# Sums of the down weight's quarters: from SBUF accumulation between products to DRAM copies and accumulating transfers during gate and up

## The chip, the cores and the metric

The program runs on one NeuronCore of one Trainium2 chip. The metric is device time in microseconds (us); less is better. The engines are named as in the profile: PE multiplies matrices (PEld is its weight load), DVE is VectorE, ACT is ScalarE, POOL is GpSimd, and SP issues most DMA transfers (SPq is its DMA queue, POOLq is POOL's).

## The reference, cut to what matters

Two decoder layers work on 512 tokens of width 1024 in float32. Each is a mixer, a layer norm, a dense SwiGLU feed-forward network (FFN) and a second layer norm. Only the FFN is touched:

```python
def swiglu(x, w_gate, w_up, w_down):
    return (jax.nn.silu(x @ w_gate) * (x @ w_up)) @ w_down
...
    for layer in range(DEPTH):
        ...
        x = layer_norm(ALPHA * x + y, ln_mix_g[layer], ln_mix_b[layer])
        x = layer_norm(ALPHA * x + swiglu(x, w_gate[layer], w_up[layer], w_down[layer]), ...)
```

The hidden width is 2816, in 22 tiles of 128 features. All weights are read from DRAM once per layer.

## The kernel before

**Products in three matmuls.** Each float32 operand is split into a rounded part `hi`, copied by ACT, and a remainder `lo`, which DVE makes as source minus `hi` (`split`, L98). A product is then three matmuls: hi by hi, hi by lo, lo by hi.

**Gate and up.** The first two hidden tiles are plain. The other twenty go in ten pairs of tiles, each by a scheme of seven block products in place of eight (`sevens`, L649). `make(i)` readies the weight operand of product i, and `take(i)` issues its 24 matmuls of 256 columns (L712). A pair of tiles needs four quarters of weight, fetched by SP into the pool `rawp`, which has `RAW` = 5 buffers of 512 KB; DVE forms the sums of quarters that the scheme needs (L684, L690).

**Down.** Sixteen of the 22 hidden tiles go through a second scheme of seven (`seven_down`, L524). There are four groups of tiles (q = 0 to 3), and for each a 2 by 2 block of weight quarters "11", "12", "21" and "22" of 512 KB each. The seven positions (`pos`) need these weights: 1 takes 11; 2 takes 21; 3 takes 22; 5 takes 11+12; 6 takes 11+12+22; 4 takes 11+12+22+21; 7 takes 22+12. That is 28 products, in the order of `seq` (L542). `make(i)` splits the weight (ACT then DVE), forms the activation combination on DVE where the position asks for one (positions 5, 6, 3 and 7, L580 to L588) and splits that too. `take(i)` issues 12 matmuls of 512 columns (L609); after the last group of a position it also copies the PSUM result away (L615, L619, L624) or combines it (L628, L631).

**Where the sums of weight quarters came from.** A buffer `tsum` in SBUF first holds quarter 11. Once `make` of position 1 has split it, POOL issues a DMA that adds quarter 12 into that same buffer (L559); once position 5 has split it, 22 is added; once position 6 has, 21. In the same way 12 is added into the buffer of 22 between positions 3 and 7. These buffers take the SBUF room of `xh` and `xl`, the split FFN input, which gate and up read to their end. The first two loads for down (quarter 21 of q = 0 and 1, at -3 and -2 in `loads`, L562) are issued inside the call of `seven_down`, before the gate and up loop goes past its seventh product.

**Order.** In the FFN the order on every engine is that of the program (`tc.manual_schedule`, L465): `make(i)`, then `take(i - AHEAD)` with `AHEAD` = 4 (L509 to L520). So what `take(i - 4)` puts on ACT and DVE stands behind what `make(i)` puts there. A split weight occupies one of `WP` = 5 pairs of buffers until its product has been taken. After the 28 products, `down` (L332) multiplies the remaining six hidden tiles plainly (L345) and runs the layer norm.

Of the kernel before, what the change touches and what calls it, by code (L numbers as in the profile page):

```python
# [10 lines left out]
F32 = mybir.dt.float32  # L11
F32R = mybir.dt.float32r
U8 = mybir.dt.uint8
AF = mybir.ActivationFunctionType
ALU = mybir.AluOpType
AX = mybir.AxisListType

P = 128
S = 512
NB = S // P  # L20
D = 1024
# [15 lines left out]
QUADS = 4  # L37
# [9 lines left out]
def trunk(ctx, tc, a, out):  # L47
    nc = tc.nc
# [7 lines left out]
    big = ctx.enter_context(tc.tile_pool(name="big", bufs=1))  # L56
    rawp = ctx.enter_context(tc.tile_pool(name="rawp", bufs=RAW))
# [4 lines left out]
    sm = ctx.enter_context(tc.tile_pool(name="sm", bufs=4))  # L62
    sm2 = ctx.enter_context(tc.tile_pool(name="sm2", bufs=2))
    sm1 = ctx.enter_context(tc.tile_pool(name="sm1", bufs=1))
    psp = ctx.enter_context(tc.tile_pool(name="psp", bufs=8, space=bass.MemoryType.PSUM))

    cnt = [0]

    def nm(s):
        cnt[0] += 1  # L70
        return f"{s}{cnt[0]}"

    def slot(dt=F32):
        return wk.tile([P, 512], dt, tag="wk", name=nm("wk"))

    def slot2(dt=F32):
        return hx.tile([P, 512], dt, tag="hx", name=nm("hx"))

    def temp(tag="tmp", dt=F32):
        return tmp.tile([P, 512], dt, tag=tag, name=nm(tag))  # L80
# [4 lines left out]
    def ps():  # L85
        return psp.tile([P, 512], F32, tag="ps", name=nm("ps"))
# [11 lines left out]
    def split(src, hi, lo, pool=False):  # L98
        nc.scalar.copy(out=hi, in_=src)  # L99
        if pool:  # L100
            n = src.shape[1] // 2
            for c in (slice(0, n), slice(n, 2 * n)):
                nc.gpsimd.tensor_tensor(out=lo[:, c], in0=src[:, c], in1=hi[:, c].bitcast(F32), op=ALU.subtract)
            return
        tt(out=lo, in0=src, in1=hi.bitcast(F32), op=ALU.subtract)  # L105
# [19 lines left out]
    xh, xl = [], []  # L125

    def renew():
        for t, n in ((xh, "xh"), (xl, "xl")):
            t[:] = [big.tile([P, 4, S], F32R, tag=f"{n}{j}", name=nm(n)) for j in range(2)]

    def xk(t, k, cols=slice(0, S)):
        return t[k // 4][:, k % 4, cols]
# [313 lines left out]
    def ffn(layer, last, flips):  # L446
        hs = []
        m8 = {}

        def hidden_tile(f):  # L450
            if f < WK:
                return slot()
            if not m8:
                m8["t"] = big.tile([P, 8, S], F32, tag="m8", name=nm("m8"))
            return m8["t"][:, f - WK, :]

        def finish(f, pg, pu):
            h = hidden_tile(f)
            t = temp()
            act(out=t, in_=pg, func=AF.Silu)  # L460
            tt(out=h, in0=t, in1=pu, op=ALU.mult)
            hs.append(h)

        E = mybir.EngineType
        with tc.manual_schedule(engines={E.PE, E.Activation, E.DVE, E.Pool, E.SP}):  # L465
            first, sx = [], {}

            def lower(flip):
                w, bank = first[-1]
                gemm_a(bank, w, cols=slice(0, 256), ks=range(4))  # L470
                if flip:
                    flips.pop(0)()
                gemm_a(bank, w, cols=slice(0, 256), ks=range(4, KD))

            def upper(f):
                for w, bank in first[2 * f:2 * f + 2]:
                    gemm_a(bank, w, cols=slice(256, 512))

            ready = state["ready"]
            for i in range(4):  # L480
                first.append((ready.pop(0), ps()))
                if i < 2:
                    ready.append(weight())
                if i == 3:
                    total, make, take, n = sevens(sx, hs, hidden_tile)
                    total(1)
                lower(i % 2)
            s1, s2_sum, s2, s3, s4 = sums(sx)
            s1()
            make(0)  # L490
            upper(0)
            finish(0, first[0][1], first[1][1])
            s2_sum()
            upper(1)
            make(1)
            make(2)
            finish(1, first[2][1], first[3][1])
            s2()
            make(3)
            take(0)  # L500
            s3()
            make(4)
            s4()
            make(5)
            take(1)
            take(2)
            make(6)
            acc, more, takes = seven_down(hs)
            for i in range(AHEAD + 3, n + len(more) + AHEAD):  # L509
                if i < n:  # L510
                    make(i)
                elif i < n + len(more):
                    more[i - n]()
                    if i == n + 3:
                        gb = load_ln("ffn", layer)
                i -= AHEAD
                if i < n:
                    take(i)
                else:
                    takes[i - n]()  # L520
        rest = [h for h in hs[:DIRECT]] + [h for h in hs[DIRECT + 2 * QUADS:]]
        return down(rest, [1, 5], gb, last, acc=acc)

    def seven_down(hs):  # L524
# [3 lines left out]
        base = state["i"]  # L528
        state["i"] += 4 * QUADS
        raw, ops = {}, {}  # L530
        t_, s_ = {}, {}

        def room(q):

            if q % 2 == 0:
                t = big.tile([P, 2, D], F32, tag=f"xh{q // 2}", name=nm("tsum"))
                s = big.tile([P, 4, 512], F32, tag=f"xl{q // 2}", name=nm("ssum"))
                for j in range(2):
                    t_[q + j], s_[q + j] = t[:, j, :], s[:, j, :]

        g = {}
        seq = [(2, 0), (2, 1), (1, 0), (1, 1), (2, 2), (5, 0), (1, 2), (5, 1), (1, 3), (2, 3), (5, 2), (6, 0),  # L542
               (5, 3), (6, 1), (6, 2), (6, 3), (3, 0), (3, 1), (3, 2), (3, 3), (7, 0), (7, 1), (7, 2), (7, 3),
               (4, 0), (4, 1), (4, 2), (4, 3)]

        def piece(which, q):
            i = base + 4 * q + ("11", "12", "21", "22").index(which)
            return a["w"][i // 2, :, (i % 2) * D:(i % 2) * D + D]

        def load(which, q):  # L550
            if which == "11":
                room(q)
                nc.sync.dma_start(out=t_[q], in_=piece(which, q))
                return
            raw[which, q] = rawp.tile([P, D], F32, tag="raw", name=nm("raw"))
            nc.sync.dma_start(out=raw[which, q], in_=piece(which, q))

        def add(t, which, q):
            nc.gpsimd.dma_start(out=t, in_=piece(which, q), accum_op=ALU.add)  # L559

        loads = {}
        for at, args in ((-3, ("21", 0)), (-2, ("21", 1)), (0, ("11", 0)), (1, ("11", 1)), (2, ("21", 2)),  # L562
                         (4, ("11", 2)), (5, ("11", 3)), (6, ("21", 3)), (12, ("22", 0)), (13, ("22", 1)),
                         (14, ("22", 2)), (15, ("22", 3))):
            loads.setdefault(at, []).append(args)

        def make(i):

            for args in loads.get(i, ()):
                load(*args)  # L570
            pos, q = seq[i]
            (a11, a21), (a12, a22) = hs[DIRECT + q], hs[DIRECT + QUADS + q]
            w = raw["21", q] if pos == 2 else raw["22", q] if pos in (3, 7) else t_[q]
            hi, lo = pair()
            split(w, hi, lo)
            if pos in (1, 5, 6, 3):
                add(w, {1: "12", 5: "22", 6: "21", 3: "12"}[pos], q)
            hh, hl = slot2(F32R), slot2(F32R)
            x = {1: a11, 2: a12, 4: a22, 7: None}.get(pos, s_.get(q))
            if pos == 5:  # L580
                tt(out=x, in0=a22, in1=a21, op=ALU.subtract)
            elif pos == 6:
                tt(out=x, in0=x, in1=a11, op=ALU.add)
            elif pos == 3:
                tt(out=x, in0=x, in1=a12, op=ALU.subtract)
            elif pos == 7:
                x = temp()
                tt(out=x, in0=a11, in1=a21, op=ALU.subtract)  # L588
            if pos == 6:
                act(out=hh, in_=x, func=AF.Copy, scale=-1.0)  # L590
                stt(out=hl, in0=x, scalar=-1.0, in1=hh.bitcast(F32), op0=ALU.mult, op1=ALU.subtract)
            else:
                split(x, hh, hl)
            ops[i] = hi, lo, hh, hl
# [38 lines left out]
        acc = {}  # L633
# [4 lines left out]
            acc.update({b: [g["a"][b], g["d"][b]] for b in range(2)})  # L638
            acc.update({b + 2: [g["f"][b], g["e"][b]] for b in range(2)})

        for at in range(-3, 0):
            for args in loads.get(at, ()):
                load(*args)
        n = len(seq)
        takes = [lambda i=i: take(i) for i in range(n)]
        takes[-1] = lambda: last(lambda: take(n - 1))
        return acc, [lambda i=i: make(i) for i in range(n)], takes

    def sevens(sx, hs, hidden_tile):  # L649

# [786 lines left out]
```

## Time and profile before

| | |
|---|---|
| three runs | 1088.09, 1090.30, 1090.39 us; median 1090.3 us |
| the profiled execution | 1089.05 us, span 1087.2 us from first to last instruction |
| PE busy (matmul) | 1049.5 us, 97% of the span |
| DVE busy | 791.2 us, 73% |
| ACT busy | 544.1 us, 50% |
| POOL busy | 89.2 us, 8% |
| mean granted PE clock | 0.986 of full speed |
| HBM read and written | 119.83 MB and 2.10 MB |

PE is busy nearly all the time, so only the places where it isn't, or where its clock is lower, can give time. Times in the rows are counted from the span's start. The down products of layer 0 run from 400 to 494 us, those of layer 1 from 953 to 1047 us.

### The profile page before, as it was taken

Reading aid. Unit: us, or ns where it says so; the run is one execution under the profiler, and the core shown is the slowest. Engines: PE = TensorE matmul, PEld = TensorE weight load, DVE = VectorE, ACT = ScalarE, POOL = GpSimd, SP = SyncE. Lnnn points to the kernel's source line nnn. Section 1 sums busy time; section 2 is a strip of 40 time slices with the busy share of each in tenths; the row PEclk is TensorE's granted clock in tenths of the full one; section 3 lists DMA queues with packets and bytes.
Section 4 is the critical chain, followed back from the end, with each engine's and each line's share of the span. In section 5 each row is a group of like instructions: output and inputs, shape, how many; then the busy total and the mean of one; then the engine's idle time right before and its main releaser. Section 6 shows DMA issues by size and latency. Waiting matters only on the chain.

```text
span 1087.2 us, 17047 instructions
## 1 busy us (share of the span) xinstructions
PE 1049.5 (97%) x6861; PEld 947.1 (87%) x6861; DVE 791.2 (73%) x1180; ACT 544.1 (50%) x896; POOL 89.2 (8%) x130
## 2 busy tenths in 40 slices
PE   9999999999999999599999999999999999997797
PEld 7888889999999997488988888889999999985686
DVE  5666549887877876685857886488887887776767
ACT  5544335655555454464467554356555554544541
POOL 0000000000000001200513411000000000022001
PEclk9999999999999999899999999999999999998899
DMA  9522222324333359833242031223424324398502
GB/s 335 201 75 79 78 78 72 97 93 129 97 102 114 98 161 256 138 101 99 97 137 77 2 117 43 78 73 79 124 90 137 97 85 130 117 255 154 133 20 78
DMA packets 35536, 123.04 MB, mean 113 GB/s; under 512 B 3952, under 2 KB 4608, under 8 KB 35456
## 3 DMA queue, kind: packets, MB, share of 16 engines
q1 hardware_dynamic: 30560, 104.12, 29.3%
q0 software_dynamic: 4896, 17.83, 9.3%
q8 instruction: 54, 0.88, 0.3%
q14 instruction: 26, 0.21, 0.1%
HBM read 119.83 MB, written 2.10 MB: 112 GB/s over the span
## 4 chain that ended last, share of the span: by engine, by line
PE 86%; DVE 5%; DMA 5%; ACT 3%; issue 1%; SPq 0%; POOL 0%; DVEq 0%; ACTq 0%; POOLq 0%
PE ps L712 35%; PE ps L189 15%; PE ps L345 13%; PE ps L609 7%; PE ps L223 6%; DMA tsum<-in_w_dram 4%; DVE w L105 2%; ACT w L99 2%; PE ps L1161 1%; PE ps L285 1%; PE ps L1086 1%; PE ps L1009 1%; PE ps L858 1%; PE ps L805 1%; PE ps L845 1%
## 5 line engine op out<-in xcount | busy, mean ns | idle before, releaser
L105 DVE TENSOR_TENSOR w<-raw,w 128x1024 fp32r<-128x1024 f32 (+2 forms) x174 | 210.0, 1211 | 60.3 <-ACT w L99 55.7
L712 PE MATMUL ps<-xh,w 128*128 128x256 f32 x1280 | 237.5, 283 | 0.0
L99 ACT CAST w<-raw 128x1024 fp32r<-128x1024 f32 (+3 forms) x177 | 181.4, 1032 | 65.7 <-PE ps L712 18.1
L712 PEld LDWEIGHTS ps<-xh,w 128*128 128x128 f32 x1280 | 202.7, 192 | 0.0
L609 PE MATMUL ps<-w,hx 128*128 128x512 f32 x672 | 159.9, 400 | 27.9 <-ACT ps L619 23.5
L712 PE MATMUL ps<-xl,w 128*128 128x256 f32 x640 | 181.1, 283 | 0.0
L609 PEld LDWEIGHTS ps<-w,hx 128*128 128x128 f32 x672 | 129.1, 193 | 58.1 <-ACT ps L619 24.4
L712 PE MATMUL ps<-hx,w 128*128 128x256 f32 x1440 | 179.6, 283 | 0.0
L712 PEld LDWEIGHTS ps<-hx,w 128*128 128x128 f32 x1440 | 176.0, 192 | 0.1
L189 PE MATMUL ps<-xh,w 128*128 128x512 f32 (+1 forms) x608 | 161.2, 348 | 0.4 <-ACT w L99 0.4
L345 PE MATMUL ps<-w,hx 128*128 128x512 f32 x657 | 151.9, 391 | 0.0
L345 PEld LDWEIGHTS ps<-w,hx 128*128 128x128 f32 x657 | 122.7, 188 | 25.1
L712 PEld LDWEIGHTS ps<-xl,w 128*128 128x128 f32 x640 | 122.8, 192 | 0.3
L189 PEld LDWEIGHTS ps<-xh,w 128*128 128x128 f32 x608 | 106.3, 189 | 15.9 <-ACT w L99 0.8
L189 PE MATMUL ps<-xl,w 128*128 128x512 f32 (+1 forms) x304 | 104.9, 345 | 0.0
L189 PEld LDWEIGHTS ps<-xl,w 128*128 128x128 f32 x304 | 57.6, 190 | 6.7 <-DVE xl L105 0.3
L559 POOL DMA_DIRECT2D tsum<-in_w_dram x24 | 20.9, 871 | 493.4 <-DVE w L105 282.1
L223 PE MATMUL ps<-w,xh 128*128 128x512 f32 (+1 forms) x192 | 58.6, 386 | 0.3 <-ACT lng L1065 0.3
L105 DVE TENSOR_TENSOR w<-tsum,w 128x1024 fp32r<-128x1024 f32 x32 | 39.2, 1224 | 18.1 <-ACT w L99 18.1
L105 DVE TENSOR_TENSOR w<-lng,w 128x1024 fp32r<-128x1024 f32 x30 | 36.7, 1223 | 17.1 <-ACT w L99 16.9
L105 DVE TENSOR_TENSOR w<-lnb,w 128x1024 fp32r<-128x1024 f32 x30 | 36.7, 1223 | 15.0 <-ACT w L99 14.9
L105 DVE TENSOR_TENSOR hx<-m,hx 128x512 fp32r<-128x512 f32 x32 | 21.4, 689 | 31.8 <-ACT hx L99 31.8
(250 smaller groups left out, 1285.4 us busy)
## 6 DMA issues: line engine op xcount, KB each, us to landing
raw<-in_w_dram SPq DMA_DIRECT2D x166, 512.0 KB, 4.3
tsum<-in_w_dram POOLq DMA_DIRECT2D x24, 512.0 KB, 8.4
raw<-in_w_dram POOLq DMA_DIRECT2D x10, 512.0 KB, 5.7
tsum<-in_w_dram SPq DMA_DIRECT2D x8, 512.0 KB, 6.3
hx<-in_xT_dram SPq DMA_DIRECT2D x8, 256.0 KB, 6.2
xn<-in_xn_dram SPq DMA_DIRECT2D x4, 512.0 KB, 9.4
out_dram<-xn SPq DMA_DIRECT2D x7, 256.0 KB, 2.0
lng<-in_ln_mix_g_dram SPq DMA_DIRECT2D x2, 512.0 KB, 7.7
```

The costliest lines, as they stand in the source:

```text
L99: nc.scalar.copy(out=hi, in_=src)
L105: tt(out=lo, in0=src, in1=hi.bitcast(F32), op=ALU.subtract)
L189: mm(dst[:, cols], lhsT=l[:, k, :], rhs=xk(r, k, cols), start=(k == 0 and n == 0), stop=(k == KD - 1 and n == 2))
L223: mm(banks[b][:, :n], lhsT=xk(l, k, t), rhs=r[:, c], start=(k == 0 and m == 0), stop=(k == KD - 1 and m == 2))
L285: nc.tensor.transpose(tp[:, k * P:(k + 1) * P], xn[:, b, h * 512 + k * P:h * 512 + (k + 1) * P], ident)
L345: mm(acc[b][h], lhsT=l(b), rhs=r[:, h * 512:h * 512 + 512], start=(not begun and k == 0 and n == 0), stop=(k == ends[b, h] and n == 2), sk ...
L559: nc.gpsimd.dma_start(out=t, in_=piece(which, q), accum_op=ALU.add)
L609: mm(bank, lhsT=l[:, t], rhs=r[:, c], start=(fresh and k == 0 and m == 0), stop=(k == 1 and m == 2), skip_group_check=True)
L712: mm(bank[:, f * 256:f * 256 + 256], lhsT=l[:, f, k, :], rhs=r[k // 2][:, k % 2, :], start=(start and f == 0 and k == 0 and m == 0), stop= ...
L805: mm(banks[s][bank][:, o:o + n], lhsT=l[rows[s], b * P:(b + 1) * P], rhs=r[rows[s], (b + 1) * P - n:(b + 1) * P], start=(i == 0), stop=(i ...
L845: nc.tensor.transpose(bank[:, o:o + P], src, ident)
L858: mm(po[rows[s], b * P:(b + 1) * P], lhsT=vn[:, j * P + 64 * s:j * P + 64 * s + 64], rhs=loc[s][(b, half)], start=(half == 0 or b == 0), s ...
```

## The change

The sums are no longer built in SBUF between products. For each q, four DRAM tiles `t` are made: t1 = 11+12, t2 = t1+22, t4 = t2+21, t3 = 22+12. Each comes from a DRAM to DRAM copy and one accumulating DMA into DRAM, both issued by POOL: 32 transfers of 512 KB per layer, kept in the list `steps`, of which one is put into the program after the `make` of gate and up product i where i % 7 is 1, 3, 5 or 6, from i = 8 on. All 28 down products then load their weight by SP into `rawp`, four products ahead, the first four from the last four gate and up products. The early loads in the call of `seven_down` are gone, as are the `tsum` buffers; of `xh` and `xl` only `xl0` is given to the activation sums.

```diff
+    dram = ctx.enter_context(tc.tile_pool(name="dram", bufs=1, space=bass.MemoryType.DRAM))
...
     def renew():
         for t, n in ((xh, "xh"), (xl, "xl")):
-            t[:] = [big.tile([P, 4, S], F32R, tag=f"{n}{j}", name=nm(n)) for j in range(2)]
+            t[:] = t or [None, None]
+            for j in range(2):
+                if t[j] is None:
+                    t[j] = big.tile([P, 4, S], F32R, tag=f"{n}{j}", name=nm(n))
...
-            acc, more, takes = seven_down(hs)
+            acc, more, takes, load, steps = seven_down(hs)
             for i in range(AHEAD + 3, n + len(more) + AHEAD):
                 if i < n:
                     make(i)
+                    if steps and i % 7 in (1, 3, 5, 6):
+                        steps.pop(0)()
+                    if i >= n - 4:
+                        load(i - n + 4)
...
-        def room(q):
-
-            if q % 2 == 0:
-                t = big.tile([P, 2, D], F32, tag=f"xh{q // 2}", name=nm("tsum"))
-                s = big.tile([P, 4, 512], F32, tag=f"xl{q // 2}", name=nm("ssum"))
...
-        def load(which, q):
-            if which == "11":
-                room(q)
-                nc.sync.dma_start(out=t_[q], in_=piece(which, q))
+        t_ = {(n, q): dram.tile([P, D], F32, tag=f"t{n}{q}", name=nm("t")) for n in (1, 2, 3, 4) for q in range(QUADS)}
+
+        def copy(n, q, src):
+            nc.gpsimd.dma_start(out=t_[n, q], in_=piece(src, q) if isinstance(src, str) else t_[src, q])
+
+        def add(n, q, which):
+            nc.gpsimd.dma_start(out=t_[n, q], in_=piece(which, q), accum_op=ALU.add)
+
+        steps = [lambda f=f, n=n, q=q, w=w: f(n, q, w)
+                 for f, n, w in ((copy, 1, "11"), (add, 1, "12"), (copy, 3, "22"), (add, 3, "12"), (copy, 2, 1),
+                                 (add, 2, "22"), (copy, 4, 2), (add, 4, "21")) for q in range(QUADS)]
+
+        def load(i):
+            if not 0 <= i < len(seq):
                 return
-            raw[which, q] = rawp.tile([P, D], F32, tag="raw", name=nm("raw"))
-            nc.sync.dma_start(out=raw[which, q], in_=piece(which, q))
-
-        def add(t, which, q):
-            nc.gpsimd.dma_start(out=t, in_=piece(which, q), accum_op=ALU.add)
-
-        loads = {}
-        for at, args in ((-3, ("21", 0)), (-2, ("21", 1)), (0, ("11", 0)), (1, ("11", 1)), (2, ("21", 2)),
-                         (4, ("11", 2)), (5, ("11", 3)), (6, ("21", 3)), (12, ("22", 0)), (13, ("22", 1)),
-                         (14, ("22", 2)), (15, ("22", 3))):
-            loads.setdefault(at, []).append(args)
+            pos, q = seq[i]
+            raw[i] = rawp.tile([P, D], F32, tag="raw", name=nm("raw"))
+            src = {1: "11", 2: "21", 3: "22", 5: 1, 6: 2, 7: 3, 4: 4}[pos]
+            nc.sync.dma_start(out=raw[i], in_=piece(src, q) if isinstance(src, str) else t_[src, q])
 
         def make(i):
 
-            for args in loads.get(i, ()):
-                load(*args)
+            load(i + 4)
+            if not s_:
+                s = big.tile([P, 4, S], F32, tag="xl0", name=nm("ssum"))
...
-            w = raw["21", q] if pos == 2 else raw["22", q] if pos in (3, 7) else t_[q]
             hi, lo = pair()
-            split(w, hi, lo)
-            if pos in (1, 5, 6, 3):
-                add(w, {1: "12", 5: "22", 6: "21", 3: "12"}[pos], q)
+            split(raw.pop(i), hi, lo)
...
-        for at in range(-3, 0):
-            for args in loads.get(at, ()):
-                load(*args)
```

## Rows read from the trace of the kernel before

**Rows 1.** Windows: window, length, each engine's busy us (instructions), PEclk, DMA share, GB/s.
```profile
219.20:392.00 172.80, 172.80 (x1442) 172.80 (x1441) 134.54 (x131) 88.97 (x114) 0.00 (x0) 1.00 0.32 101
400.40:459.70 59.30, 45.04 (x194) 35.51 (x192) 39.97 (x49) 28.26 (x39) 13.10 (x15) 0.94 0.94 203
```

**Rows 2.** Timeline of PE, both down stages: start, us, instructions merged, [idle before, releaser].
```profile
400.44 30.11 PE L609 MATMUL ps<-w,hx 128*128 128x512 f32 x132
432.70 11.58 PE L609 MATMUL ps<-w,hx 128*128 128x512 f32 x48 [2.15 <-ACT tmp L624]
...
459.73 34.45 PE L609 MATMUL ps<-w,hx 128*128 128x512 f32 x144 [11.97 <-ACT ps L619]
...
952.64 30.11 PE L609 MATMUL ps<-w,hx 128*128 128x512 f32 x132
984.78 15.49 PE L609 MATMUL ps<-w,hx 128*128 128x512 f32 x60 [2.03 <-ACT tmp L624]
1011.81 34.86 PE L609 MATMUL ps<-w,hx 128*128 128x512 f32 x144 [11.54 <-ACT ps L619]
```

**Rows 3.** Timeline of ACT, both down stages: weight splits of products, columns as before.
```profile
415.45 1.05 ACT L99 CAST w<-tsum 128x1024 fp32r<-128x1024 f32 x1
...
416.92 1.04 ACT L99 CAST w<-raw 128x1024 fp32r<-128x1024 f32 x1
...
421.08 1.05 ACT L99 CAST w<-tsum 128x1024 fp32r<-128x1024 f32 x1 [2.60 <-DMA tsum<-in_w_dram]
...
428.59 1.06 ACT L99 CAST w<-tsum 128x1024 fp32r<-128x1024 f32 x1 [0.47 <-DMA tsum<-in_w_dram]
...
971.90 1.05 ACT L99 CAST w<-tsum 128x1024 fp32r<-128x1024 f32 x1 [1.36 <-PE ps L609]
...
980.68 1.05 ACT L99 CAST w<-tsum 128x1024 fp32r<-128x1024 f32 x1 [1.74 <-DMA tsum<-in_w_dram]
```

**Rows 4.** Timeline of POOL, both layers: two of its DMA issues, columns as before.
```profile
398.27 0.88 POOL L559 DMA_DIRECT2D tsum<-in_w_dram  x1 [211.09 <-DVE w L105]
...
963.33 0.87 POOL L559 DMA_DIRECT2D tsum<-in_w_dram  x1 [3.61 <-DVE w L105]
```

**Rows 5.** DMA issues in 963:965, 263.4:263.8 and 403.7:404.2; last number: us to landing.
```profile
tsum<-in_w_dram POOLq DMA_DIRECT2D x1, 512.0 KB, 8.5
...
raw<-in_w_dram SPq DMA_DIRECT2D x1, 512.0 KB, 6.1
...
raw<-in_w_dram SPq DMA_DIRECT2D x1, 512.0 KB, 24.3
```

**Rows 6.** Timeline of SP's queue in gate and up of layer 0.
```profile
210.50 0.33 SPq L556 DMA_DIRECT2D raw<-in_w_dram  x1
...
262.40 0.33 SPq L665 DMA_DIRECT2D raw<-in_w_dram  x1
...
263.53 0.33 SPq L665 DMA_DIRECT2D raw<-in_w_dram  x1
```

**Rows 7.** Timeline of DVE in gate and up, and in down, of layer 0.
```profile
269.74 1.23 DVE L690 TENSOR_TENSOR lng<-raw,raw 128x1024 f32<-128x1024 f32 x1 [1.67 <-DMA raw<-in_w_dram]
...
272.02 1.22 DVE L690 TENSOR_TENSOR lnb<-lng,raw 128x1024 f32<-128x1024 f32 x1
...
476.67 1.22 DVE L105 TENSOR_TENSOR w<-tsum,w 128x1024 fp32r<-128x1024 f32 x1
```

**Rows 8.** Timeline of ACT: the second weight split of the plain tiles after the scheme.
```profile
486.06 1.06 ACT L99 CAST w<-raw 128x1024 fp32r<-128x1024 f32 x1 [0.67 <-PE ps L609]
```

**Rows 9.** DMA queues over the span: packets, MB, share of 16 engines (q0 is POOL's).
```profile
q1 hardware_dynamic: 30560, 104.12, 29.3%
q0 software_dynamic: 4896, 17.83, 9.3%
```

**Rows 10.** The DMA view of 398.2:428.5: everything moved, and POOL's transfers among it.
```profile
DMA packets 2070, 7.59 MB, mean 251 GB/s; under 512 B 221, under 2 KB 221, under 8 KB 2068
...
tsum<-in_w_dram POOLq DMA_DIRECT2D x8, 512.0 KB, 9.6
```

More of the change, by code (lines that the diff above doesn't have):

```diff
@@ L530, in seven_down @@
         raw, ops = {}, {}
-        t_, s_ = {}, {}
-        def room(q):
-            if q % 2 == 0:
-                t = big.tile([P, 2, D], F32, tag=f"xh{q // 2}", name=nm("tsum"))
-                s = big.tile([P, 4, 512], F32, tag=f"xl{q // 2}", name=nm("ssum"))
-                for j in range(2):
-                    t_[q + j], s_[q + j] = t[:, j, :], s[:, j, :]
+        s_ = {}
         g = {}
@@ new lines, in load @@
+        def load(i):
+            if not 0 <= i < len(seq):
+                return
+            pos, q = seq[i]
+            raw[i] = rawp.tile([P, D], F32, tag="raw", name=nm("raw"))
+            src = {1: "11", 2: "21", 3: "22", 5: 1, 6: 2, 7: 3, 4: 4}[pos]
+            nc.sync.dma_start(out=raw[i], in_=piece(src, q) if isinstance(src, str) else t_[src, q])
+        def make(i):
+            load(i + 4)
+            if not s_:
+                s = big.tile([P, 4, S], F32, tag="xl0", name=nm("ssum"))
+                s_.update({q: s[:, q, :] for q in range(QUADS)})
+                xl[0] = None
@@ L646, in seven_down @@
         takes[-1] = lambda: last(lambda: take(n - 1))
-        return acc, [lambda i=i: make(i) for i in range(n)], takes
+        return acc, [lambda i=i: make(i) for i in range(n)], takes, load, steps
     def sevens(sx, hs, hidden_tile):
```

## The prediction, made before the change was run

> **What bounds the kernel now.** I read the share of each engine first: PE is the bound, so a gain can only come from places where PE stands or runs at a lower clock. The windows by stage come next. In gate and up PE has no gap: 172.80 of 172.80 us at full clock, with the DMA engines 0.32 busy [rows 1]. In the first 59.30 us of the down products PE works 45.04 us, at a mean clock of 0.94, with the DMA engines at 0.94 [rows 1]. So the change can win in the down products and lose in gate and up.
>
> The timeline of PE then gives the size. The first 132 matmuls of down take 30.11 us, 0.228 us each, so a product (12 matmuls) takes 2.737 us, and 28 would take 76.6 us. They take from 400.44 to 459.73 + 34.45 = 494.18, 93.7 us: 17.1 us are lost in layer 0, and in the same way 94.03 - 76.6 = 17.4 us in layer 1 [rows 2]. Most of it is one gap per layer, 11.97 and 11.54 us, before the last 144 matmuls (the last 12 products), and PE waits there for a copy on ACT (L619), not for a DMA [rows 2].
>
> Why that copy is late decides the prediction. L619 belongs to `take(15)`, the last of position 6: it copies away the bank into which `take(16)` goes on adding, so `take(16)` has to wait for it. In ACT's order it stands behind `make(19)`. So PE waits for the chain of makes on ACT and DVE, whatever feeds it. Here the waits for the DMAs enter: product 10's weight split begins at 421.08 after 2.60 us of waiting for an accumulating transfer, product 12's at 428.59 after 0.47 [rows 3]. In layer 1 the split of product 10 is put down to PE (1.36 us), but that of product 12 to the DMA (1.74) [rows 3]. I read the first as a DMA too: POOL issued the addition that this sum needs at 963.33 [rows 4], it landed 8.5 us later [rows 5], at 971.83, and the split began at 971.90.
>
> **The change, step by step.**
>
> *The waits for the sums.* Nothing then holds `make` but its buffers: five pairs, so `make(10)` may begin when `take(5)` ends, 6 products after the start: 400.44 + 6 x 2.737 = 416.86. Can the makes before it keep up? A make with an activation sum takes half of 428.59 - 0.47 - 421.08, 3.52 us; one without, 416.92 - 415.45 = 1.47 us [rows 3]. `make(5)` may start when `take(0)` ends, at 403.2; products 5 and 7 are long, 6, 8 and 9 short: 403.2 + 2 x 3.52 + 3 x 1.47 = 414.6. They can.
>
> *The chain that stays.* Products 10 to 23 are all long, and 3.52 us is more than PE's 2.737. From the start of `make(10)` to the start of `take(16)` there are 459.73 - 421.08 = 38.65 us, 38.18 without the DMA wait; in layer 1 1011.81 - 971.90 - 1.74 = 38.17 [rows 2, 3]. This stretch holds ten makes and the copies between them, none of which the change touches. So `take(16)` starts at 416.86 + 38.18 = 455.04, 4.7 us earlier than 459.73; in layer 1 (times of before) at 952.64 + 16.42 + 38.17 = 1007.23, 4.6 us earlier than 1011.81. The small gap of 2.15 and 2.03 us closes [rows 2], but PE only comes earlier to the large one: `take(15)` then ends at 400.44 + 16 x 2.737 = 444.2, and the gap is 10.8 us, hardly less than 11.97. That closed gap is therefore not added. Together 9.3 us.
>
> *Bounds of that term.* If the 1.36 us in layer 1 really was PE, at the end of `take(6)`, `make(10)` starts one product, 2.74 us, later in both layers, and 3.8 us remain. If the gap became short enough that the last 144 matmuls ran at 0.228 in place of 34.45/144 = 0.239 us, 1.6 us come on top in each layer. With a gap of 10.8 us I don't expect that.
>
> *28 loads by SP in place of 12.* That is 16 more issues of 0.33 us a layer [rows 6] on a queue with little to do. Each load is issued when the split five products earlier is done, four makes ahead of its own: at least 4 x 1.47 = 5.9 us if all are short, above 11 us at PE's pace. A load in gate and up landed in 6.1 us with two others in flight [rows 5], so I cost it at nothing. Without that cover each late load would delay a make by its lateness. The plain tiles behind the scheme lose their early loads: the second one gets the buffer of product 24, freed at 476.67 + 1.22 = 477.9 [rows 7], lands 6.1 us later at 484.0, and is split at 486.06 [rows 8]; both move forward together. Nothing.
>
> *32 POOL transfers a layer, in place of 16.* POOL's issues take 0.87 us each, 28 us, and POOL stood idle for 211.09 us before its first addition [rows 4], so nobody stands behind them. They have no wait for the makes beside which they are written: the copies depend on nothing, the additions on the copy or the sum before. So they run in a burst at the start of gate and up. Of the eight groups of four, each waits at most for the landing of an earlier one; with the 9.6 us of additions in a crowd [rows 10], 8 x 9.6 + 28 = 105 us, half of the 211. No load of down waits for them.
>
> *What the burst does to gate and up.* Engine time from the queues: plain transfers 29.3% of 1087.2 us for 104.12 MB, 1.60 us for 512 KB; POOL's 9.3% for 17.83 MB, 2.97 us [rows 9]. The best row for the crowd is the start of down: in 30.3 us 7.59 MB were moved [rows 10], some 15 transfers, 8 of them additions, 2.0 us each. Turn about, a load then takes some 4 us, and the four loads of a pair of tiles 16 of the 20.16 us that PE needs for its 7 products (7 x 2.88). That fits. An addition into DRAM isn't in the trace: from below it costs the 2.97 us of one into SBUF, from above 5.94 us, if reading the old value from DRAM doubles it. I take 2.97, the nearest row: same queue, same operation.
>
> *Two buffers given back.* The early loads for down, one of them at 210.50 [rows 6], occupy two of the five `rawp` buffers through all of gate and up. The rows show it: the load issued at 263.53 lands 6.1 us later, at 269.63, and DVE has waited 1.67 us for it at 269.74 [rows 5 to 7]. PE didn't feel it, so there is no gain. But with five buffers each load takes the buffer freed two releases earlier: the second sum's load would be issued by 262.40 for use at 272.02 [rows 6, 7], 9.6 us for a transfer of some 4 us plus its latency. This is cover against the burst.
>
> **The sum.** 1089.05 - 4.7 - 4.6 = 1079.8 us against the profiled execution; the median of before is 1.25 us above that execution, so 1081 us. Its own range: 3.2 us less (1077) to 5.5 more (1086.5).
>
> **Rivals.**
>
> *The whole stall goes.* If PE waited for data alone, all 17.1 + 17.4 us would come back: 1056. The gap names ACT and not a DMA, and ten makes at 3.5 us can't be fed to PE at 2.737. Chance 0.05.
>
> *No change.* The waits return as late plain loads, each product's load depending on a buffer that the makes themselves free. Then 1089 to 1091. Against it stand the 11 us of cover. Chance 0.1.
>
> *Slower: the burst starves gate and up.* Let all DRAM traffic share the 327 GB/s at which plain loads run (104.12 MB in 318.5 us of engine time [rows 9]). An addition in DRAM reads twice and writes once, 1.57 MB, 4.8 us; turn about with 1.60 us loads a pair of tiles needs 4 x 6.4 = 25.6 us where PE needs 20.16. Sixteen additions cover four pairs: 21.8 us, less the lead of four products (11.5 us), 10.3 us a layer, and 1081 + 20.6 = 1102. At 5.94 us an addition it would be 1138. It decides from 4.45 us per addition on, where the loss equals the gain. For it: one load issued in the crowd took 24.3 us [rows 5]. Against: that one stood behind seven others in SP's queue. Chance 0.15.
>
> The Trainium skill speaks here too (DMA: Bandwidth & Descriptors, "Bandwidth"): it gives about 358 GB/s as one core's share of HBM when both cores of a stack stream, which would make an addition 4.4 us and the time 1089, an estimate from that page. The trace of before does not settle it: nothing in it reads and writes DRAM together at a high rate.
>
> **How the numbers follow.** The forecast has 0.7. A measurement tells 0.2%, some 2 us, from no change: faster means below 1088. Faster takes the forecast and the first rival, 0.75; same 0.1; slower 0.15. The range from 1074 to 1096 holds the forecast, the second rival and the mild part of the third, and leaves out the first and the rest of the third.
>
> **What would show it.** Right: PE in gate and up still without gap; `make(10)`'s split about 16.5 us after PE's first down matmul (now 20.6); no wait of a weight split for a DMA in down; the wait at L624 gone; the wait at L619 still 10 to 11 us; `take(16)` 54.6 us after the first down matmul (now 59.3); and the DMA share in gate and up clearly above 0.32, most of all early. Wrong: gaps of L712 in gate and up with ACT or DVE waiting for `raw`; a wait at L619 of a few us or none; splits in down that wait for plain loads.

## The result, and the profile after

| | before | after |
|---|---|---|
| median | 1090.35 us (1088.09 to 1090.76, 4 runs) | 1081.15 us (1080.37 to 1082.31, 4 runs) |
| profiled execution | 1089.05 us, span 1087.2 | 1080.37 us, span 1078.6 |

The ratio of the runs after to those before is 0.9921, with a 95% interval from 0.9903 to 0.9938: 0.8% faster. The prediction said 1081.

The page after, its first lines, the DMA queues and the traffic of HBM:

```profile
span 1078.6 us, 17142 instructions
...
PE 1046.4 (97%) x6861; PEld 946.5 (88%) x6861; DVE 792.5 (73%) x1180; ACT 543.4 (50%) x896; POOL 103.5 (10%) x162
...
q1 hardware_dynamic: 35168, 120.89, 33.1%
q0 software_dynamic: 7712, 34.61, 12.7%
...
HBM read 153.38 MB, written 35.65 MB: 175 GB/s over the span
```

The work of PE is the same 6861 matmuls, and the span is 8.6 us shorter. Of these, 3.1 us stand as busy time of PE (1049.5 us before), all in the matmuls of down (159.9 us before, 156.8 after); the rest is idle time. Part of the 3.1 us is the clock: right behind the small gap of layer 1, which is gone now, the mean granted clock was 0.58 of full speed, mostly the lower of its two levels (1.2 GHz). The row of before (columns as in [rows 1]):

```profile
984.80:987.50 2.70, 2.70 (x7) 2.17 (x8) 1.47 (x3) 1.37 (x2) 0.00 (x0) 0.58 1.03 179
```

The timeline of PE in the two down stages, to be laid beside [rows 2]:

```profile
400.55 43.71 PE L613 MATMUL ps<-w,hx 128*128 128x512 f32 x192
455.23 35.11 PE L613 MATMUL ps<-w,hx 128*128 128x512 f32 x144 [10.97 <-ACT ps L623]
...
948.51 43.71 PE L613 MATMUL ps<-w,hx 128*128 128x512 f32 x192
1003.18 34.27 PE L613 MATMUL ps<-w,hx 128*128 128x512 f32 x144 [10.96 <-ACT ps L623]
```

The first 192 matmuls now run without a gap, where there was one of some 2 us behind the first 132. The large gap stays, 10.97 and 10.96 us for 11.97 and 11.54, and it names the same copy (L619 is now L623). From the first down matmul to the 193rd there are 54.68 and 54.67 us, for 59.29 and 59.17 [rows 2]: 4.6 and 4.5 us less.

The weight split of product 10 on ACT, which waited for a DMA [rows 3], and the copy that releases PE:

```profile
417.14 1.05 ACT L100 CAST w<-raw 128x1024 fp32r<-128x1024 f32 x1 [1.15 <-issue]
...
454.60 1.06 ACT L623 COPY ps<-ps 128x512 f32<-128x512 f32 x2
...
965.10 1.05 ACT L100 CAST w<-raw 128x1024 fp32r<-128x1024 f32 x1 [1.14 <-issue]
```

In both layers the split begins 16.59 us after the first down matmul, for 20.64 and 19.26 before, and between it and the copy no weight split of down waits for a DMA. The copy still comes last.

The work went into gate and up. POOL's first and last issue there, and the DMA queues and issues from 187 to 272 us, the issues with the median time to landing:

```profile
187.02 2.44 POOL L554 DMA_DIRECT2D t<-in_w_dram  x4
...
264.80 0.81 POOL L557 DMA_DIRECT2D t<-in_w_dram  x1 [0.98 <-DMA t<-t]
```

```profile
q0 software_dynamic: 3637, 16.54, 76.0%
q1 hardware_dynamic: 2079, 7.60, 24.8%
...
t<-in_w_dram POOLq DMA_DIRECT2D x24, 512.0 KB, 11.0
raw<-in_w_dram SPq DMA_DIRECT2D x17, 512.0 KB, 10.2
t<-t POOLq DMA_DIRECT2D x8, 512.0 KB, 12.8
```

The 32 transfers are issued within 78 us of a stage that lasts some 200, as a burst. SP's 17 loads beside it land in 10.2 us in the median. Before, 16 loads of the same stretch took 4.0:

```profile
raw<-in_w_dram SPq DMA_DIRECT2D x16, 512.0 KB, 4.0
```

The windows in and behind the burst (columns as in [rows 1]):

```profile
220.00:250.00 30.00, 30.00 (x252) 30.00 (x252) 24.77 (x25) 15.86 (x20) 7.74 (x12) 1.00 1.04 285
250.00:280.00 30.00, 30.00 (x252) 30.00 (x252) 23.63 (x24) 14.59 (x19) 4.43 (x7) 1.00 0.98 290
...
310.00:340.00 30.00, 30.00 (x252) 30.00 (x252) 23.77 (x24) 14.84 (x19) 0.00 (x0) 1.00 0.26 89
```

In the burst the DMA engines are full (shares of 1.04 and 0.98), and PE has no gap and full clock.

### The profile page after: what moved, and what is told of

It is laid out like the page before. It is cut to its first block, busy times and chain, and to the rows that moved or that the text cites. A ratio compares the mean times of both kernels' runs of the same rounds, so it can differ in the third digit from the quotient of the medians.

```text
span 1078.6 us, 17142 instructions
## 1 busy us (share of the span) xinstructions
PE 1046.4 (97%) x6861; PEld 946.5 (88%) x6861; DVE 792.5 (73%) x1180; ACT 543.4 (50%) x896; POOL 103.5 (10%) x162
## 3 DMA queue, kind: packets, MB, share of 16 engines
q0 software_dynamic: 7712, 34.61, 12.7%
HBM read 153.38 MB, written 35.65 MB: 175 GB/s over the span
## 4 chain that ended last, share of the span: by engine, by line
PE 90%; DVE 5%; ACT 3%; issue 1%; DMA 0%; SPq 0%; POOL 0%; DVEq 0%; ACTq 0%; POOLq 0%
PE ps L713 37%; PE ps L193 16%; PE ps L349 13%; PE ps L613 9%; PE ps L227 6%; DVE w L106 2%; ACT w L100 2%; PE ps L1162 1%; PE ps L289 1%; PE ps L1087 1%; PE ps L1010 1%; PE ps L859 1%; PE ps L806 1%; PE ps L846 1%; PE ps L1060 0%
## 5 line engine op out<-in xcount | busy, mean ns | idle before, releaser
L106 DVE TENSOR_TENSOR w<-raw,w 128x1024 fp32r<-128x1024 f32 (+2 forms) x206 | 249.2, 1214 | 77.3 <-ACT w L100 72.2
L100 ACT CAST w<-raw 128x1024 fp32r<-128x1024 f32 (+3 forms) x209 | 215.0, 1035 | 79.2 <-PE ps L713 17.0
L613 PE MATMUL ps<-w,hx 128*128 128x512 f32 x672 | 156.8, 396 | 21.9 <-ACT ps L623 21.9
L349 PE MATMUL ps<-w,hx 128*128 128x512 f32 x657 | 151.9, 391 | 0.0
L266 POOL TENSOR_TENSOR rs<-ve,neghalf 128x1 f32<-128x1 f32 x15 | 9.2, 611 | 713.5 <-DVE ve L264 675.2
L227 PEld LDWEIGHTS ps<-w,xh 128*128 128x128 f32 x192 | 35.2, 188 | 5.0
```

What stands on the lines that cost most here:

```text
L227: mm(banks[b][:, :n], lhsT=xk(l, k, t), rhs=r[:, c], start=(k == 0 and m == 0), stop=(k == KD - 1 and m == 2))
L349: mm(acc[b][h], lhsT=l(b), rhs=r[:, h * 512:h * 512 + 512], start=(not begun and k == 0 and n == 0), stop=(k == ends[b, h] and n == 2), sk ...
L613: mm(bank, lhsT=l[:, t], rhs=r[:, c], start=(fresh and k == 0 and m == 0), stop=(k == 1 and m == 2), skip_group_check=True)
```

## The experiments

**Theory.** The gain is the waits of product 10 and its neighbours for the accumulating transfers; the gap that stays is the chain of makes on ACT and DVE; the burst is hidden by gate and up, and the two buffers given back are part of what hides it. **Rivals.** The gain comes from the freed buffers; the burst has a price that the gain hides; the gap belongs to the place of the copy or to the waits for the DMAs, not to the chain.

**e1: no sums at all.** The kernel leaves out every copy and addition; the down products load single quarters.

```diff
-        t_ = {(n, q): dram.tile(...) ...}
...
+        steps = []
...
-            src = {1: "11", 2: "21", 3: "22", 5: 1, 6: 2, 7: 3, 4: 4}[pos]
+            src = {1: "11", 2: "21", 3: "22", 5: "12", 6: "22", 7: "12", 4: "21"}[pos]
...
```

> The changed kernel without any copy or accumulating transfer: the down products load single quarters, so the sums of quarters are left out of the computation. My theory (the burst of POOL transfers is wholly hidden in gate and up): 1081 us, within 1 us of the changed kernel, gap before the last 144 down matmuls still 10 to 11 us. Rival (the burst has a price that the gain hides): 1078 us or less.

Measured: 1080.6 us (1079.66 to 1081.4), ratio to before 0.9915 [0.9902, 0.9929], for 0.9921 [0.9903, 0.9938] with the sums. Without any sum the down stages look the same:

```profile
401.31 43.71 PE L602 MATMUL ps<-w,hx 128*128 128x512 f32 x192
455.98 35.38 PE L602 MATMUL ps<-w,hx 128*128 128x512 f32 x144 [10.96 <-ACT ps L612]
```

So the sums cost nothing that can be measured here, and the gap stays without them. Nor does any split or sum of gate and up in layer 0 wait for a load in this kernel: its 17 loads from 187 to 272 us land in 4.3 us in the median, so it is the burst that makes them late.

**e2: the kernel before, with the two buffers given back.**

```diff
                 if i < n:
                     make(i)
+                    if n - 4 <= i < n - 2:
+                        early[i - n + 4]()
...
-        for at in range(-3, 0):
-            for args in loads.get(at, ()):
-                load(*args)
+        early = [lambda args=args: load(*args) for at in range(-3, 0) for args in loads.get(at, ())]
...
```

> The kernel before, with nothing changed but its two early down loads: they are issued from two of the last four gate and up products, so that all five raw buffers serve gate and up. My theory (the freed buffers give no time by themselves): 1090 us, no change. Rival (part of the gain comes from the freed buffers): 1086 us or less.

Measured: 1089.4 us (1087.43 to 1091.75, 11 runs), ratio 0.9996 [0.9987, 1.0005]: no change. The waits of DVE's sums in gate and up [rows 7] are gone from its trace, and nothing is won by it. The freed buffers don't explain the gain.

**e3: the changed kernel, with the two buffers held again.**

```diff
-                    if i >= n - 4:
+                    if i >= n - 2:
                         load(i - n + 4)
...
+        load(0)
+        load(1)
         n = len(seq)
```

> The changed kernel, with its first two down loads issued as early as before, so that they hold two of the five raw buffers through gate and up while the burst runs. My theory (the five buffers are the cover against the burst): with three buffers the loop of load, sum, split and next load is some 17 us of the 20.16 us of a pair, and loads slower by 3 to 6 us push it beyond, so gate and up shows gaps of PE and the time is 1082 to 1095 us. Rival (the lead of four products is cover enough): 1081 us and no gap in gate and up.

Measured: 1112.21 us (1110.23 to 1112.59), ratio 1.0202 [1.0188, 1.0216]: 31 us slower than the changed kernel, from the time of issue of two loads. That is the direction of the theory, but far above its 1082 to 1095 us: the size was missed. The windows of the burst in this kernel, one sum of DVE, and the down products:

```profile
220.00:250.00 30.00, 24.36 (x186) 24.15 (x185) 16.82 (x17) 8.84 (x11) 7.78 (x12) 0.89 1.04 277
250.00:280.00 30.00, 25.13 (x195) 24.73 (x195) 17.78 (x18) 13.69 (x18) 4.39 (x7) 0.94 0.84 228
280.00:310.00 30.00, 30.00 (x252) 30.00 (x252) 23.89 (x24) 16.55 (x22) 0.00 (x0) 1.00 0.41 134
```

```profile
239.30 1.23 DVE L693 TENSOR_TENSOR lng<-raw,raw 128x1024 f32<-128x1024 f32 x1 [11.35 <-DMA raw<-in_w_dram]
```

```profile
415.32 43.71 PE L613 MATMUL ps<-w,hx 128*128 128x512 f32 x192
469.98 35.55 PE L613 MATMUL ps<-w,hx 128*128 128x512 f32 x144 [10.96 <-ACT ps L623]
...
978.43 43.71 PE L613 MATMUL ps<-w,hx 128*128 128x512 f32 x192
```

PE stands idle for 10.5 us in two windows, and its mean granted clock there falls to 0.89 and 0.94 of full speed; a sum waits 11.35 us for a load, where one of before waited 1.67 [rows 7]. As soon as the burst ends, PE is full again. The first down matmul comes at 415.32 in place of 400.55, in layer 1 at 978.43 in place of 948.51: 14.8 us lost in the first layer and 15.2 in the second. What follows is unchanged: the gap behind the 192 matmuls is 10.96 us here too. So the burst is not free by itself: it is covered, and the cover is the two buffers.

**e6: every copy and addition twice.**

```diff
                         steps.pop(0)()
+                        steps.pop(0)()
...
-        t_ = {... for n in (1, 2, 3, 4) for q in range(QUADS)}
+        t_ = {... for n in (1, 2, 3, 4, 5, 6, 7, 8) for q in range(QUADS)}
...
+                                 (copy, 5, "11"), (add, 5, "12"), (copy, 7, "22"), (add, 7, "12"), (copy, 6, 5),
+                                 (add, 6, "22"), (copy, 8, 6), (add, 8, "21")) for q in range(QUADS)]
```

> The changed kernel with every copy and addition made a second time into spare DRAM tiles that nobody reads: 64 POOL transfers a layer. My theory (SP's loads get their share of the DMA engines whatever POOL has queued): the burst lasts some 170 us in place of 85, PE in gate and up stays without gap, 1081 to 1083 us. Rival (the crowd eats a lead that more time would use up): gaps in the second half of gate and up and 1090 us or more.

Measured: 1080.87 us (1080.37 to 1081.0), ratio 0.9917 [0.9903, 0.9931]: as without the second set. POOL's last issue, the loads and transfers from 187 to 360 us, and two windows:

```profile
354.86 0.81 POOL L558 DMA_DIRECT2D t<-in_w_dram  x1 [0.64 <-DMA t<-t]
```

```profile
t<-in_w_dram POOLq DMA_DIRECT2D x48, 512.0 KB, 12.8
raw<-in_w_dram SPq DMA_DIRECT2D x33, 512.0 KB, 11.7
```

```profile
280.00:310.00 30.00, 30.00 (x252) 30.00 (x251) 22.65 (x22) 15.78 (x21) 7.83 (x11) 1.00 1.01 299
310.00:340.00 30.00, 30.00 (x252) 30.00 (x251) 24.08 (x24) 14.48 (x20) 6.58 (x10) 1.00 1.05 292
```

Loads that land in 11.7 us for 170 us on end don't starve PE. With five buffers the cover is no reserve that runs down: the loads are issued early enough.

**e4: the activation sum ahead of the weight split.** One block of `make` in the changed kernel is moved up; nothing else.

```diff
             (a11, a21), (a12, a22) = hs[DIRECT + q], hs[DIRECT + QUADS + q]
-            hi, lo = pair()
-            split(raw.pop(i), hi, lo)
-            hh, hl = slot2(F32R), slot2(F32R)
             x = {1: a11, 2: a12, 4: a22, 7: None}.get(pos, s_.get(q))
             if pos == 5:
                 tt(out=x, in0=a22, in1=a21, op=ALU.subtract)
...
                 tt(out=x, in0=a11, in1=a21, op=ALU.subtract)
+            hi, lo = pair()
+            split(raw.pop(i), hi, lo)
+            hh, hl = slot2(F32R), slot2(F32R)
             if pos == 6:
```

> The changed kernel with one thing moved: in the make of a down product the activation sum on DVE stands ahead of the weight split, so it runs while ACT copies the weight. Nothing is left out. My theory (the gap that stays is the chain of makes): a long make takes about 2.45 us of DVE in place of 3.5 us of the two engines in turn, less than PE's 2.74, the gap before the last 144 matmuls shrinks to under 2 us, and the time is 1056 to 1062 us. Rival (the gap belongs to the copy of the bank and PE's own order): 1078 us or more.

Measured: 1054.8 us (1054.51 to 1054.94), ratio to before 0.9676 [0.966, 0.9692], 1.2 us below the expected range. The timeline of PE, and of DVE for one long make:

```profile
400.82 76.35 PE L613 MATMUL ps<-w,hx 128*128 128x512 f32 x336
...
935.66 76.35 PE L613 MATMUL ps<-w,hx 128*128 128x512 f32 x336
```

```profile
420.24 0.68 DVE L584 TENSOR_TENSOR ssum<-ssum,wk 128x512 f32<-128x512 f32 x1
421.21 1.23 DVE L106 TENSOR_TENSOR w<-raw,w 128x1024 fp32r<-128x1024 f32 x1 [0.29 <-ACT w L100]
422.36 0.69 DVE L595 SCALAR_TENSOR_TENSOR hx<-ssum,hx 128x512 fp32r<-128x512 f32 x1
422.96 0.69 DVE L582 TENSOR_TENSOR ssum<-m,wk 128x512 f32<-128x512 f32 x1
```

All 336 matmuls run without a gap, 76.35 us in each layer, the 76.6 that the prediction had put down as the floor. From one activation sum to the next there are 2.72 us where a long make took 3.5, and 0.29 of them DVE waits; some 2.45 us were expected, but 2.72 is no more than PE's 2.737. The gap was the chain. This kernel, which beats both, is the version that the experiments point to.

**e5: the same move in the kernel before.** The diff is that of e4, on the kernel before (with the addition by POOL moved along behind the split).

> The kernel before with the same move of the activation sum. My theory: the chain is shortened here too, but the waits for the accumulating transfers stay and now set the pace of the makes from product 5 to 15; 1062 to 1074 us, slower than the changed kernel with this move by 5 to 14 us. Rival (the DMA waits alone made the gap of before): 1086 us or more.

Measured: 1069.12 us (1068.48 to 1070.25), ratio 0.981 [0.9795, 0.9824]. The rival falls: the waits for the DMAs alone did not make the gap. Two of the five such waits of ACT in layer 0, and PE:

```profile
422.14 1.05 ACT L99 CAST w<-tsum 128x1024 fp32r<-128x1024 f32 x1 [5.06 <-DMA tsum<-in_w_dram]
429.76 1.05 ACT L99 CAST w<-tsum 128x1024 fp32r<-128x1024 f32 x1 [3.43 <-DMA tsum<-in_w_dram]
```

```profile
431.86 13.91 PE L609 MATMUL ps<-w,hx 128*128 128x512 f32 x60 [0.96 <-ACT tmp L624]
450.16 35.28 PE L609 MATMUL ps<-w,hx 128*128 128x512 f32 x144 [4.39 <-ACT ps L619]
```

With the chain shortened what is left to wait for is the accumulating transfers (13.7 us in these five waits), and the change is worth 1069.12 - 1054.8 = 14.3 us, more than the 9 us that it brings by itself (the expectation had 5 to 14).

**e7: the takes of products 12 to 15 behind `make(16)`.**

```diff
+                elif i - n == 15 - 3:
+                    for j in range(12, 16):
+                        takes[j]()
-                else:
+                elif not 12 < i - n < 16:
                     takes[i - n]()
```

> The changed kernel with the takes of products 12 to 15 put into the program behind the make of product 16, so that the copies of position 6 stand on ACT behind that make and no longer behind that of product 19. Nothing is left out. My theory (the makes of products 10 to 23 are slower than PE, wherever the copy stands): product 16 starts some 10 us earlier, but PE then waits a little before each product up to 23, and 4 to 6 us are won in both layers together: 1075 to 1078 us. Rival (the place of the copy alone costs the gap): 1062 us or less.

Measured: 1081.61 us (1080.25 to 1082.1), ratio 0.9921 [0.9906, 0.9936]: no gain, where 4 to 6 us were expected. The timeline of PE from product 16 on:

```profile
445.08 3.01 PE L616 MATMUL ps<-w,hx 128*128 128x512 f32 x12 [0.59 <-ACT ps L626]
449.05 3.29 PE L616 MATMUL ps<-w,hx 128*128 128x512 f32 x12 [0.95 <-ACT hx L100]
...
469.83 3.29 PE L616 MATMUL ps<-w,hx 128*128 128x512 f32 x12 [0.17 <-ACT hx L100]
477.13 12.78 PE L616 MATMUL ps<-w,hx 128*128 128x512 f32 x48 [4.01 <-ACT ps L626]
```

Product 16 does start 10 us earlier, and the rival falls, because the gap only comes out elsewhere: the products follow each other every 3.46 us, the pace of a long make, and before product 24 PE waits 4.01 us for the copies of position 7, which stand behind `make(27)`. I had left out that second copy. The 28 products end at 489.91, for 490.34 in the changed kernel.

## Why the prediction was right, step by step

*The waits for the sums.* Right, and in size: 4.7 and 4.6 us were predicted to the start of product 16, 4.61 and 4.50 came. Product 10's split starts 16.59 us after the first down matmul, 16.5 predicted, in both layers; in layer 1 it started 19.26 us after it before [rows 2, 3], so the wait put down to PE there was the DMA. The last 144 matmuls give 0.66 us back in layer 0 (35.11 for 34.45, at a mean granted clock of 0.93 for 0.95) and win 0.59 in layer 1 (0.96 for 0.94). The prediction had expected no change there; that the two cancel is luck.

*The chain that stays.* Right: from the start of `make(10)` to that of `take(16)` there are 38.09 and 38.08 us, for 38.18 and 38.17 reckoned. A gap of 10.8 us was predicted, 10.97 and 10.96 were measured, named by the same copy. e4 shows that it is the chain and e7 that it isn't the place of the copy. The rival "the whole stall goes" asked for 1056, and got it only once the chain was shortened as well (e4).

*28 loads by SP.* Right: no split of down waits for one between products 10 and 19, and without any burst (e1) the time is the same.

*The burst and gate and up.* The outcome is right, a term of it was too small. I had reckoned that a load in the crowd takes some 4 us and had set its lateness against a cover of 9.6; loads land in 10.2 us in the median of the burst. The rate was not the error (50 transfers in the 85 us from 187 to 272, 1.7 us each, for 2.0 reckoned). As I read it, a load stands beside others in SP's queue and takes turns with POOL's, of which several are in flight; no run separates the two. Some splits in gate and up do wait, 3.89 us at most on ACT in layer 0, and PE has no gap, so the lead of the makes over PE absorbs it. That the burst did no harm rests on this lead and the buffers, not on loads of 4 us.

*Two buffers given back.* Called cover and costed at nothing: right (e2), and it is what decides the sign. The rival "the burst starves gate and up" is what happens without them (e3, 1112 us, beside the 1102 worked out for it), though by late loads rather than by dear additions. Its condition, over 4.45 us for each addition, isn't met. From 265 to 280 us only additions were left in POOL's queue; its packets, MB and share of that window:

```profile
q0 software_dynamic: 485, 1.74, 58.8%
```

That is 2.66 us per 512 KB, no more than the 2.97 of an addition into SBUF [rows 9], which the prediction had taken. What the prediction gave in its favour has a slip: the load that took 24.3 us stood behind six others in SP's queue, not seven. Two more slips of the prediction change nothing: 3.2 us under 1081 is 1078 and not 1077, and four makes at PE's pace are 10.9 us of cover, not above 11.

The Trainium skill (DMA: Bandwidth & Descriptors, "Bandwidth") gives about 358 GB/s as a core's share of HBM when both cores of a stack stream; an estimate from it was 4.4 us for an addition and 1089 us. On this one core that didn't come about: an addition took 2.66 us, and twice the transfers (e6) still leave the time at 1081. In the 85 us of the burst the queues moved 16.54 MB (POOL, all but 0.52 of it written to DRAM as well as read) and 7.60 MB (SP), some 470 GB/s of DRAM reads and writes together, an estimate from these bytes. With both cores of a stack at work it wasn't tried.

## What to carry to other kernels

When PE waits for a copy that stands behind the work of preparing later products, compare that work's time per product with PE's before you speed up what feeds it: removing the DMA waits won 9 us of some 35, and starting an independent sum before the operation that waits for another engine won 26 more. Transfers moved under a busy stage are free only as long as that stage's own loads are issued early enough to land later than before; count the buffers that something else holds meanwhile. And a change that removes one wait may be worth more with the next bound gone (9 us alone, 14 beside e4).

## What the runs showed that I had not expected

Additions into DRAM cost the DMA engines no more than additions into SBUF: 2.66 us per 512 KB where only additions were left in POOL's queue, for 2.97 in the kernel before, whose additions all went into SBUF [rows 9]. Copies within DRAM and additions together take 2.07 us in the mean over the span (12.7% of 1078.6 us for 34.61 MB). And the profile's HBM bytes don't hold the reading of the old values: 153.38 - 119.83 = 33.55 MB more were read, which are just the 64 further transfers of 0.524 MB by their source.
